# Two transformer layers on one core: transfers of the mixer's solve in a fixed order, solves and Sin moved, inverse roots of the second stage as GpSimd powers

## The chip, the cores and the metric

The kernel runs on one core of one Trainium2 chip. A core has five engines with a queue of instructions each: TensorE (PE, matmuls), VectorE (DVE), ScalarE (ACT), GpSimd (POOL) and SyncE (SP, which here only issues transfers). They meet at semaphores, and 16 DMA engines move data between DRAM and the on-chip memory. The metric is the device time of one execution in microseconds (us); lower is better. The median of three runs before is 1295.21 us (1294.62 to 1304.61).

## What is computed

512 rows of 1024 features go through two layers in fp32. The first layer mixes the sequence in two halves of the features, retention and RWKV7, then attends to a memory of 256 rows and applies a squared-ReLU MLP; the second is a gated hybrid of grouped attention and a spatial MLP. Cut to what the change touches:

```python
def wkv7_scan(r, w, k, v, a_vec, b_vec):            # 8 heads of 64, 512 steps
    def step(state, inp):
        sa = jnp.einsum('bhvk,bhk->bhv', state, a_t)
        state = (state * w_t[:, :, None, :] + sa[..., None] * b_t[:, :, None, :]
                 + v_t[..., None] * k_t[:, :, None, :])
        return state, jnp.einsum('bhvk,bhk->bhv', state, r_t)
...
def first_block(x, mem, positions, ...):
    p = rmsnorm(x, norm_mix) @ w_in
    y = concat([retention_mixer(p[:RET], positions), rwkv7_mixer(p[RET:])])   # retention turns q, k by sin, cos
    x = x + y @ w_out
    x = x + memory_cross_attention(rmsnorm(x, norm_xattn), rmsnorm(mem, norm_mem), ...)
    h = rmsnorm(x, norm_mlp)
    x = x + jnp.square(jax.nn.relu(h @ mlp_w_up)) @ mlp_w_down
    return rmsnorm(x, norm_final)

def hybrid_layer(x, ...):
    z = rmsnorm_2(x, norm_gain) @ w_in               # q, k, v, gate_a, u, v, gate_b, g_merge
    q = axial_rope(rmsnorm_2(q per head, q_gain)); k = axial_rope(rmsnorm_2(k per head, k_gain))
    attn = block_attention(q, k, v) * silu(gate_a)
    gm = gelu(u) * spatial(layernorm(gelu(v))) * silu(gate_b)
    y = sigmoid(g0) * (attn @ w_proj_attn) + sigmoid(g1) * (gm @ w_proj_gmlp)
    return x + y @ w_out                             # then a last rmsnorm_2
```

## The kernel before

**Matmuls.** Each weight unit of 128x1024 is fetched by SP (L285, `raw`), cast on ScalarE to a rounded high part `wh` (L295) and subtracted to a low part `wl` (L296) on VectorE, or on GpSimd for the units that `lowpart` names. A product takes three matmuls, high by high, high by low and low by high; most have 128x512 columns.

**Who sets the order.** TensorE's order is that in which the Python code calls `self.T` (class `Ordered` ties each instruction behind the last). The code is a main generator and side generators that `streams` runs in turns: at each `yield` the main one has emitted a step, mostly four matmuls of 128x512, and a side generator that yields n comes back n steps later. The other engines' order is set by the scheduler that places instructions.

**The mixer.** The RWKV7 half treats 512 steps as 16 chunks of 32, eight per half (`hf` 0 and 1). `side(hf)` runs `products` (chunk matrices `gs`, whose corners go through DRAM by the writes of L1595 into `dm`), `invert` (L1624: both halves of `dm` are read; L1630 and L1632: 31 elimination steps on GpSimd; L1637 to L1646: the inverse goes to DRAM as `d1` and `dw` and comes back as `sv` and as diagonal blocks of `gs`), then waits `self.wait[hf]` steps, then `solve` (two products, F and W, per half matrix, with copies on ScalarE at L1659 and L1666), then `chain`: for each chunk the xy product, the copy `xs` (L1684), steps of other matmuls, the us product, the copy L1690, and the state products. Chain 0 runs from 164 to 205 us. The `trig` generator makes sine and cosine of the retention's angles on GpSimd and ScalarE (L704); they are needed by the retention part, which follows.

**Norms.** `rsqrt` (L357 to L366) is a first guess from the bits and three Newton steps on VectorE: nine instructions for one column, twelve for several. The first stage's own row norms use one GpSimd power (`rs`, L477). Users in the change: `norm_scale` (last norm), the turn of the attention's and the MLP's rows (`turn`, L1002), `fin` at the end of the MLP (L1156 to L1170), `heads` (L1231 to L1243, ten heads of a row block) and `layer_norm` (L1291 to L1300).

Of the kernel before, what the change touches and what calls it, by code (L numbers as in the profile page):

```python
# [16 lines left out]
P = 128  # L17
# [212 lines left out]
class Kern:  # L230
    def __init__(self, ctx, tc, A, out):
        self.tc, self.nc, self.A, self.out = tc, tc.nc, A, out
        self.T = Ordered(tc, tc.nc.tensor)
        pool = lambda name, **k: ctx.enter_context(tc.tile_pool(name=name, bufs=1, **k))
        self.cp = pool("cp")
        self.wp = pool("wp")
        self.tp = pool("tp")
        self.sp = pool("sp")
        self.sm = pool("sm")
        self.dp = pool("dp", space=bass.MemoryType.DRAM)  # L240
        self.nraw = self.nspl = 0
        self.raw, self.spl = {}, {}
        self.NU = A["wst"].shape[0]
        self.u = 0
        self.cnt = 0
        self.nh = 3
        self.lowpart = lambda u: u <= 3 or 55 <= u < 79 or 145 <= u
        self.wait = [33, 25]

# [103 lines left out]
    def rsqrt(self, x, n, p0=0, p1=P, tag="sm", V=None):  # L353
# [13 lines left out]
        return y  # L367

    def rms(self, xb, junk, eps=1e-6):

        nc = self.nc
        ss = self.small(1)
        nc.scalar.activation(junk, xb, AF.Square, accum_out=ss)
        v = self.small(1)
        nc.vector.tensor_scalar(v, ss, 1.0 / D, eps, op0=ALU.mult, op1=ALU.add)
        return self.rsqrt(v, 1)
# [65 lines left out]
    def first(self):  # L442
# [29 lines left out]
        v = self.small(4)  # L472
        rs, mh = self.small(4), self.small(4)
        G.memset(mh, -0.5)
# [182 lines left out]
    def trig(self):  # L657
# [42 lines left out]
        for x, o in ((acc, self.sin), (w, self.cos)):  # L700
            V.tensor_scalar(o, x, -0.4999999, 0.4999999, op0=ALU.max, op1=ALU.min)
        yield 95
        for o in (self.sin, self.cos):
            nc.scalar.activation(o, o, AF.Sin, scale=2.0 * math.pi)  # L704

# [266 lines left out]
    def turn_half(self, st, b, j, ps, dst, delay):  # L972
# [10 lines left out]
        def turn():  # L983
# [13 lines left out]
            if b == NB - 1:  # L997
                yield 5
                v = self.small(4)
                nc.vector.tensor_reduce(v, st["ss"].rearrange("p (b j) -> p b j", j=2), axis=AX.X, op=ALU.add)  # L1000
                nc.vector.tensor_scalar(v, v, 1.0 / D, 1e-6, op0=ALU.mult, op1=ALU.add)
                st["scale"](self.rsqrt(v, 4))  # L1002

        self.spawn(turn(), delay)

    def norm_scale(self, ss, scale=1.0 / D, eps=1e-6):
        V = self.nc.vector
        v = self.small(1)
        V.tensor_reduce(v, ss, axis=AX.X, op=ALU.add)
        V.tensor_scalar(v, v, scale, eps, op0=ALU.mult, op1=ALU.add)  # L1010
        return self.rsqrt(v, 1)

# [95 lines left out]
    def mlp(self):  # L1108
# [15 lines left out]
        def main():  # L1124
# [28 lines left out]
            def fin(b):  # L1153
# [6 lines left out]
                V.scalar_tensor_tensor(c1, a1, 1.0 / D, a0, op0=ALU.mult, op1=ALU.add)  # L1160
                rs = self.rsqrt(c1, 1)
                xg = self.tmp((P, 1024), "t4", 2)
# [5 lines left out]
                self.flags.add(f"norm {b}")  # L1168
                rs = self.rsqrt(c0, 1)
                V.tensor_scalar(self.x[b], self.x[b], rs, None, op0=ALU.mult)  # L1170
# [18 lines left out]
    def second(self):  # L1189
# [32 lines left out]
        def heads(b):  # L1222
# [9 lines left out]
            V.tensor_scalar(ss, ss, 1.0 / 64, 1e-6, op0=ALU.mult, op1=ALU.add)  # L1232
            rn = self.rsqrt(ss, 10)
            V.tensor_tensor(x3, x3, rn.unsqueeze(2).broadcast_to([P, 10, 64]), op=ALU.mult)
# [53 lines left out]
        def layer_norm(b):  # L1288
# [6 lines left out]
            V.tensor_scalar(e, mv[:, 1:2], 0.25, 1e-6, op0=ALU.mult, op1=ALU.add)  # L1295
            rs = self.rsqrt(e, 1)
            V.tensor_scalar(rs, rs, 0.5, None, op0=ALU.mult)
# [274 lines left out]
    def products(self, hf, sl):  # L1572
# [7 lines left out]
        for c in range(0, 8, 2):  # L1580
# [10 lines left out]
            if c % 4 == 2:  # L1591
                q = c // 4
                for b in range(2):
                    r = 32 * b + 16 * q
                    nc.sync.dma_start(dm[r:r + 16].rearrange("p s t -> s p t"),  # L1595
                                      gs[q][32 * b:32 * b + 32, :, :, 32 * b:32 * b + 32].rearrange("s c h t -> s (c h) t"))
# [13 lines left out]
    def invert(self, hf, sl):  # L1610
# [22 lines left out]

        d1, dw = self.dram(32), self.dram()
        for e in range(2):
            o = slice(64 * e, 64 * e + 32)
            G.tensor_copy(m[o, :, 0:16], w[o].rearrange("p i t -> p t i"))  # L1637
            nc.sync.dma_start(d1[:, :, 16 * e:16 * e + 16], m[o, :, 0:16])
        for e, o in enumerate(half):
            nc.sync.dma_start(dw.rearrange("p (i e) t -> p i e t", e=2)[:, :, e], w[o])  # L1640
        sv = m[0:32]
        nc.sync.dma_start(sv, d1.rearrange("p t c -> t p c"))
        for b in range(2):
            for q in range(2):
                r = 32 * b + 16 * q
                nc.sync.dma_start(gs[q][32 * b:32 * b + 32, :, :, 32 * b:32 * b + 32].rearrange("s c h t -> s (c h) t"),  # L1646
                                  dw[r:r + 16].rearrange("p c t -> c p t"))
        sl["fw"] = sv, m[32:64]

    def solve(self, hf, sl):  # L1650
# [11 lines left out]
        for q in range(2):  # L1662
            wp = self.psum("cs", (32, 16, 32))
            for i in range(16):
                self.T.matmul(wp[:, i], f[:, q * 16 + i], gs[q][32:64, i // 4, i % 4, 32:64], start=True, stop=True)
            SC.copy(gs[q][0:32, :, :, 32:64], wp.rearrange("p (c h) t -> p c h t", h=4))  # L1666
        yield 2

    def chain(self, hf, sl):
# [5 lines left out]
        for c in range(8):  # L1675
# [8 lines left out]
            SC.copy(xs, xy[0:64])  # L1684
            yield 2
            us = self.psum("ch")
# [64 lines left out]
```

## Time and profile before

| what | before |
|---|---|
| runs (us) | 1304.61, 1295.21, 1294.62; median 1295.21 |
| profiled execution (us) | 1293.28, of which the span is 1291.5 |
| TensorE busy | 1243.6 us (96%), 6976 instructions |
| VectorE, ScalarE, GpSimd busy | 690.8 (53%), 511.2 (40%), 455.5 us (35%) |
| mean granted clock of TensorE | 0.988 of full speed |
| mixer / attention and MLP / second layer | 0 to about 390 / to 930 / to 1291 us |

The time is that of one profiled execution. An engine is busy while an instruction of it runs; a wait is the idle time ahead of an instruction, put down to what released it. TensorE has two clock levels, 1.2 and 2.4 GHz, and the granted clock of a stretch is the mean over it as a share of 2.4 GHz.

### The profile page before, as it was taken

To read this page: it belongs to the slowest core of one execution; us is meant where nothing else is said; L and a number is where in the kernel's file an instruction comes from. 1 tells how busy PE (TensorE), PEld (TensorE's weight loads), DVE (VectorE), ACT (ScalarE), POOL (GpSimd) and SP (SyncE) were. 2 spreads that over 40 slices of the span, in tenths; PEclk is the share of its full clock that TensorE was granted. 3 is DMA by queue.
4 is the path that set the end of the run, shared out by engine and by line. 5 is a ranking of instruction groups with operands and counts; after the bars stand their busy time and mean duration, and the time that the engine had idled before them with its cause. 6 is when DMAs were issued, how large, how long until landed. Compare 5 with 4: busy or idle time off the path is not lost.

```text
span 1291.5 us, 18137 instructions
## 1 busy us (share of the span) xinstructions
PE 1243.6 (96%) x6976; PEld 1027.9 (80%) x6976; DVE 690.8 (53%) x1455; ACT 511.2 (40%) x921; POOL 455.5 (35%) x490
## 2 busy tenths in 40 slices
PE   7999699999999999999999999999999999999997
PEld 6767578887888898798888888888787878787886
DVE  5767323557784555444333333334869856564455
ACT  5453133332354544444322232234444435455232
POOL 5917572244210242235210111012314763222574
PEclk9999799999999999999999999999999999999999
DMA  6222414111245232223333323243232231221321
GB/s 207 75 57 82 98 43 109 50 37 63 90 139 187 60 97 82 82 66 114 98 98 98 95 91 96 96 123 97 93 98 65 83 114 51 64 66 50 114 82 66
DMA packets 52089, 115.49 MB, mean 89 GB/s; under 512 B 23169, under 2 KB 23809, under 8 KB 52002
## 3 DMA queue, kind: packets, MB, share of 16 engines
q1 hardware_dynamic: 51824, 114.25, 29.6%
q8 instruction: 55, 0.90, 0.3%
q14 instruction: 32, 0.26, 0.1%
q10 hardware_dynamic: 146, 0.07, 0.0%
q0 software_dynamic: 32, 0.00, 0.0%
HBM read 110.90 MB, written 3.41 MB: 89 GB/s over the span
## 4 chain that ended last, share of the span: by engine, by line
PE 79%; POOL 7%; DVE 6%; ACT 4%; issue 2%; DMA 2%; SPq 0%; ACTq 0%; DVEq 0%; POOLq 0%
PE mm L221 36%; PE cs L221 32%; PE ch L221 7%; PE tp L221 4%; POOL s L221 3%; POOL o L1630 1%; POOL s L1632 1%; ACT wh L295 1%; DVE wl L296 1%; DMA raw<-wst 1%; DMA s<-dm 1%; DVE s L887 1%; ACT t L1102 0%; DVE t L1104 0%; DMA dm<-s 0%
## 5 line engine op out<-in xcount | busy, mean ns | idle before, releaser
L221 PE MATMUL mm<-s,wh 128*128 128x512 f32 (+1 forms) x880 | 263.3, 379 | 2.2 <-DVE t L542 2.0
L295 ACT CAST wh<-raw 128x1024 fp32r<-128x1024 f32 x151 | 158.6, 1051 | 255.8 <-PE mm L221 197.8
L221 PE MATMUL mm<-wh,s 128*128 128x512 f32 (+1 forms) x824 | 229.2, 347 | 1.2 <-DVE t L719 0.8
L296 DVE TENSOR_TENSOR wl<-raw,wh 128x1024 fp32r<-128x1024 f32 x99 | 123.2, 1244 | 171.3 <-ACT wh L295 170.8
L221 PEld LDWEIGHTS mm<-s,wh 128*128 128x128 f32 x880 | 159.0, 190 | 37.5 <-issue 7.2
L296 POOL TENSOR_TENSOR wl<-raw,wh 128x1024 fp32r<-128x1024 f32 x52 | 125.7, 2420 | 134.5 <-ACT wh L295 123.2
L221 PEld LDWEIGHTS mm<-wh,s 128*128 128x128 f32 x824 | 146.5, 191 | 22.1 <-PE mm L221 1.2
L221 PE MATMUL mm<-s,wl 128*128 128x512 f32 (+1 forms) x432 | 163.1, 378 | 1.0 <-DVE wl L221 1.0
L221 PE MATMUL cs<-s,wh 128*128 128x512 f32 (+1 forms) x544 | 154.2, 366 | 0.0
L221 PE MATMUL mm<-wl,s 128*128 128x512 f32 (+1 forms) x412 | 140.7, 342 | 2.5 <-POOL wl L296 2.5
L221 PE MATMUL cs<-wh,s 128*128 128x512 f32 (+1 forms) x440 | 143.0, 389 | 0.0
L1120 POOL TENSOR_TENSOR t<-t 128x512 f32<-128x512 f32 x32 | 49.9, 1559 | 217.0 <-ACT t L1119 217.0
L221 PEld LDWEIGHTS cs<-s,wh 128*128 128x128 f32 x544 | 97.8, 189 | 16.2 <-issue 0.2
L221 PE MATMUL cs<-s,wl 128*128 128x512 f32 (+1 forms) x272 | 99.7, 366 | 0.0
L221 PEld LDWEIGHTS cs<-wh,s 128*128 128x128 f32 x440 | 82.5, 190 | 16.4
L221 PEld LDWEIGHTS mm<-s,wl 128*128 128x128 f32 x432 | 81.8, 189 | 14.7 <-DVE wl L221 1.2
L296 POOL TENSOR_TENSOR wlx<-raw,whx 128x1024 fp32r<-128x1024 f32 x17 | 41.3, 2428 | 136.4 <-ACT whx L295 133.2
L221 PEld LDWEIGHTS mm<-wl,s 128*128 128x128 f32 x412 | 78.9, 191 | 11.5 <-POOL wl L296 2.9
L221 PE MATMUL cs<-wl,s 128*128 128x512 f32 (+1 forms) x220 | 85.5, 389 | 0.0
L351 DVE TENSOR_TENSOR s<-t,s 128x512 fp32r<-128x512 f32 x44 | 34.8, 790 | 64.1 <-ACT s L350 64.0
L221 PE MATMUL ch<-s,s 128*64 128x64 f32 (+3 forms) x504 | 61.1, 268 | 4.8 <-ACT s L1690 2.4
L295 ACT CAST whx<-raw 128x1024 fp32r<-128x1024 f32 x35 | 36.6, 1047 | 66.4 <-PE mm L221 48.1
(312 smaller groups left out, 2128.6 us busy)
## 6 DMA issues: line engine op xcount, KB each, us to landing
raw<-wst SPq DMA_DIRECT2D x189, 512.0 KB, 3.7
s<-x SPq DMA_DIRECT2D x8, 512.0 KB, 5.7
s<-rows SPq DMA_DIRECT2D x4, 512.0 KB, 4.2
out<-t SPq DMA_DIRECT2D x8, 256.0 KB, 2.3
t<-mem SPq DMA_DIRECT2D x2, 512.0 KB, 3.9
dm<-s SPq DMA_DIRECT2D x10, 64.0 KB, 2.3
s<-dm SPq DMA_DIRECT2D x2, 256.0 KB, 4.1
s<-dm SPq DMA_DIRECT2D x8, 64.0 KB, 2.5
```

The source lines that it names most:

```text
L221: r = getattr(self.eng, name)(*a, **k)
L295: (SC or nc.scalar).copy(h, r)
L296: (E or (nc.gpsimd if self.lowpart(self.nspl) else nc.vector)).tensor_tensor(l, r, h.bitcast(F32), op=ALU.subtract)
L351: self.nc.vector.tensor_tensor(dst[1], src, dst[0].bitcast(F32), op=ALU.subtract)
L887: (V or self.nc.vector).tensor_tensor(dst[1], ps, dst[0].bitcast(F32), op=ALU.subtract)
L1120: nc.gpsimd.tensor_tensor(q, r, r, op=ALU.mult)
L1630: G.tensor_tensor(tv, w[:, 0:k, s:s + 1].broadcast_to([P, k, n]), m[:, s:s + 1, s + 1:32].broadcast_to([P, k, n]), op=ALU.mult)
L1632: G.tensor_tensor(w[:, 0:k, s + 1:32], w[:, 0:k, s + 1:32], tv, op=ALU.add)
```

## The change

- `self.wait` becomes [40, 16]: solve 0 starts seven steps later behind its products, solve 1 nine steps earlier.
- The Sin and Cos of L704 wait for the flag "solve 0" and are tied behind the last copy of the W product.
- The chunk writes of L1595 go to ScalarE's queue, in the order of the code.
- The transfers around the inverse are issued on SP in a fixed order: both `dw`, both `d1`, two reads of diagonal blocks, `sv`, two reads.
- In half 0 the chain yields one step fewer between `xs` and the us product.
- `power` replaces `rsqrt` at 22 places outside the mixer: a GpSimd `tensor_tensor` with the operation pow and a tile of -0.5.

```diff
-        self.wait = [33, 25]
+        self.wait = [40, 16]
...
+    def power(self, x, n):
+        y = self.small(n)
+        self.nc.gpsimd.tensor_tensor(y, x, self.half[:, 0:n], op=ALU.pow)
         return y
...
-        rs, mh = self.small(4), self.small(4)
+        rs = self.small(4)
+        mh = self.half = self.cp.tile([P, 10], F32, name="half")
         G.memset(mh, -0.5)
...
         yield 95
+        yield "solve 0"
         for o in (self.sin, self.cos):
-            nc.scalar.activation(o, o, AF.Sin, scale=2.0 * math.pi)
+            r = nc.scalar.activation(o, o, AF.Sin, scale=2.0 * math.pi)
+            self.tc.add_manual_dep(r.ins, self.mark.ins.name, mybir.DependencyInfo(
+                mybir.DependencyClass.NoSync, mybir.DependencyReason.DATA), reason="order of the instructions")
...
-                st["scale"](self.rsqrt(v, 4))
+                st["scale"](self.power(v, 4))
...
-                rs = self.rsqrt(c1, 1)
+                rs = self.power(c1, 1)
...
-            rn = self.rsqrt(ss, 10)
+            rn = self.power(ss, 10)
...
-                    nc.sync.dma_start(dm[r:r + 16].rearrange("p s t -> s p t"),
+                    SC.dma_start(dm[r:r + 16].rearrange("p s t -> s p t"),
...
+        Q = Ordered(self.tc, nc.sync)
+        for e, o in enumerate(half):
+            Q.dma_start(dw.rearrange("p (i e) t -> p i e t", e=2)[:, :, e], w[o])
         for e in range(2):
             o = slice(64 * e, 64 * e + 32)
             G.tensor_copy(m[o, :, 0:16], w[o].rearrange("p i t -> p t i"))
-            nc.sync.dma_start(d1[:, :, 16 * e:16 * e + 16], m[o, :, 0:16])
-        for e, o in enumerate(half):
-            nc.sync.dma_start(dw.rearrange("p (i e) t -> p i e t", e=2)[:, :, e], w[o])
+            Q.dma_start(d1[:, :, 16 * e:16 * e + 16], m[o, :, 0:16])
         sv = m[0:32]
-        nc.sync.dma_start(sv, d1.rearrange("p t c -> t p c"))
         for b in range(2):
             for q in range(2):
...
-                nc.sync.dma_start(gs[q][32 * b:32 * b + 32, :, :, 32 * b:32 * b + 32].rearrange("s c h t -> s (c h) t"),
+                Q.dma_start(gs[q][32 * b:32 * b + 32, :, :, 32 * b:32 * b + 32].rearrange("s c h t -> s (c h) t"),
...
+            if b == 0:
+                Q.dma_start(sv, d1.rearrange("p t c -> t p c"))
...
-            SC.copy(gs[q][0:32, :, :, 32:64], wp.rearrange("p (c h) t -> p c h t", h=4))
+            self.mark = SC.copy(gs[q][0:32, :, :, 32:64], wp.rearrange("p (c h) t -> p c h t", h=4))
...
             SC.copy(xs, xy[0:64])
-            yield 2
+            yield 1 + hf
```

The same replacement of `rsqrt` by `power` stands in `norm_scale`, in `fin` for c0 and in `layer_norm`. Line numbers of the kernel after are larger by 6 to 12.

**SP at solve 0.** `dm_1004` is `dw` of half 0, `dm_1003` its `d1`, `s_156_904` (after: `s_155_904`) the tile that holds `sv`, and `s_126`, `s_127` (`s_125`, `s_126`) are the two chunk matrices. First SP's row before:

```order
L1640 DMA dm_1004<-s_156_904 1024x1x32 x2
L1638 DMA dm_1003<-s_156_904 1024x1x16
L1646 DMA s_126_757<-dm_1004 32x16x32
L1646 DMA s_127_758<-dm_1004 32x16x32
L1646 DMA s_126_757<-dm_1004 32x16x32
L1638 DMA dm_1003<-s_156_904 1024x1x16
L1646 DMA s_127_758<-dm_1004 32x16x32
L1595 DMA dm_1294<-s_240_1292 32x16x32 x2
L1642 DMA s_156_904<-dm_1003 32x32x32
```

Now, in the changed kernel:

```order
L221 DMA dm_1004<-s_155_904 1024x1x32 x2
L221 DMA dm_1003<-s_155_904 1024x1x16 x2
L221 DMA s_125_757<-dm_1004 32x16x32
L221 DMA s_126_758<-dm_1004 32x16x32
L221 DMA s_155_904<-dm_1003 32x32x32
L221 DMA s_125_757<-dm_1004 32x16x32
L221 DMA s_126_758<-dm_1004 32x16x32
L285 DMA raw_1519<-wst 128x1024
```

Both parts of `d1` moved ahead of the reads, `sv` ahead of the last two, and the writes for the second half (L1595) left SP's row. TensorE's row at the same place, before, with the F matmuls of solve 0 (`cs_1526`, `cs_1544`):

```order
L221 MATMUL mm_1349<-s_12_106,wh_1241 128x512
L221 MATMUL mm_1349<-s_14_108,wh_1241 128x512
L221 MATMUL mm_1349<-s_12_106,wl_1242 128x512
L221 MATMUL cs_1526<-s_156_904,s_126_757 32x32 x16
L221 MATMUL cs_1544<-s_156_904,s_127_758 32x32 x16
L221 MATMUL mm_1525<-s_11_105,wh_1282 128x512
```

and now (`cs_1564`, `cs_1582`):

```order
L221 MATMUL mm_1525<-s_12_106,wl_1282 128x512
L221 MATMUL mm_1559<-s_11_105,wh_1345 128x512
L221 MATMUL mm_1559<-s_13_107,wh_1345 128x512
L221 MATMUL mm_1559<-s_11_105,wl_1346 128x512
L221 MATMUL mm_1559<-s_11_105,wh_1345 128x512
L221 MATMUL cs_1564<-s_155_904,s_125_757 32x32 x16
L221 MATMUL cs_1582<-s_155_904,s_126_758 32x32 x16
```

The 24 matmuls into `mm_1525` and four into `mm_1559` moved ahead of the solve.

**ScalarE from solve 0 to chunk 0.** Before, the row from the W copies (L1666) to the copy of the us product (L1690):

```order
L1666 COPY s_126_757<-cs_1570 32x16x32
L1666 COPY s_127_758<-cs_1588 32x16x32
L1684 COPY xs_1619<-ch_1614 64x256
L1606 COPY s_308_1621<-cs_1622 128x4x128
L1606 COPY s_308_1621<-cs_1628 128x4x128
L295 CAST wh_1647<-raw_1343 128x1024
L764 ACTIVATE t_1642<-mm_1525 128x512
L1690 COPY s_42_280<-ch_1652 64x256
```

Now, the same stretch (L1678 are the W copies, L1696 `xs`, L1702 the copy of the us product):

```order
L1678 COPY s_126_758<-cs_1626 32x16x32
L712 ACT_TABLE_LOAD
L712 ACTIVATE sin<-sin 128x128
L712 ACTIVATE cos<-cos 128x128
L1696 COPY xs_1657<-ch_1652 64x256
L1616 COPY s_312_1659<-cs_1660 128x4x128
L1616 COPY s_312_1659<-cs_1666 128x4x128
L295 CAST wh_1681<-raw_1519 128x1024
L774 ACT_TABLE_LOAD
L774 ACTIVATE t_1676<-mm_1559 128x512
L1702 COPY s_41_280<-ch_1688 64x256
```

Sin, Cos and two table loads came in; the three loads that stood further ahead, around L704, L1467 and L1459, are gone from the row.

**GpSimd at `heads`.** `L1242` and `L1243` (after: L1252 and L1253) make the rotated queries and keys of a row block. Before:

```order
L1242 TENSOR_TENSOR s_1390_8233<-t_1470_8687,t_1471_8688 128x20x16
L1243 TENSOR_TENSOR s_1390_8233<-t_1470_8687,t_1471_8688 128x20x16
L296 TENSOR_TENSOR wl_8766<-raw_8647,wh_8765 128x1024
L296 TENSOR_TENSOR wlx_8836<-raw_8717,whx_8835 128x1024
L1242 TENSOR_TENSOR s_1391_8234<-t_1490_8803,t_1491_8804 128x20x16
L1243 TENSOR_TENSOR s_1391_8234<-t_1490_8803,t_1491_8804 128x20x16
L296 TENSOR_TENSOR wl_8883<-raw_8763,wh_8882 128x1024
```

Now:

```order
L1252 TENSOR_TENSOR s_1377_8167<-t_1445_8555,t_1446_8556 128x20x16
L1253 TENSOR_TENSOR s_1377_8167<-t_1445_8555,t_1446_8556 128x20x16
L296 TENSOR_TENSOR wl_8634<-raw_8528,wh_8633 128x1024
L372 TENSOR_TENSOR sm_8655<-sm_8652,half 128x10
L296 TENSOR_TENSOR wlx_8691<-raw_8585,whx_8690 128x1024
L1252 TENSOR_TENSOR s_1378_8168<-t_1463_8658,t_1464_8659 128x20x16
L1253 TENSOR_TENSOR s_1378_8168<-t_1463_8658,t_1464_8659 128x20x16
L296 TENSOR_TENSOR wl_8738<-raw_8631,wh_8737 128x1024
```

The power of row block 2 stands ahead of a weight split, `wlx`, and the split that follows the queries keeps its place.

## Rows read from the trace of the kernel before

**Rows 1.** TensorE's waits, 60 to 320 us: waiter, released by, total us, times, longest

```profile
PE cs L221 <- DMA s<-dm: 9.4, 1, 9.4
PE ch L221 <- ACT s L1690: 2.4, 3, 1.1
...
PE mm L221 <- DVE t L542: 2.0, 1, 2.0
```

**Rows 2.** TensorE's waits, 900 to 1292 us

```profile
PE tp L221 <- DVE t L1165: 2.5, 1, 2.5
PE mm L221 <- POOL wl L296: 2.5, 1, 2.5
```

**Rows 3.** Windows: stretch, length; busy us of PE, PEld, DVE, ACT, POOL; clock, DMA share, GB/s

```profile
60.00:80.00 20.00, 18.05 (x86) 13.44 (x84) 13.56 (x20) 11.91 (x17) 6.98 (x12) 0.91 0.26 73
...
180.00:200.00 20.00, 17.79 (x158) 14.45 (x156) 11.54 (x25) 6.42 (x15) 16.02 (x34) 1.00 0.30 70
...
900.00:950.00 50.00, 46.73 (x213) 37.79 (x212) 38.34 (x128) 21.62 (x57) 13.20 (x25) 0.97 0.28 84
950.00:1000.00 50.00, 47.53 (x260) 40.77 (x259) 42.03 (x103) 21.45 (x37) 17.59 (x12) 1.00 0.32 102
```

**Rows 4.** Timeline of GpSimd: start, us, engine, line, operation, out<-in

```profile
141.91 2.24 POOL L1637 COPY s<-s 32x512 f32<-32x512 f32 x2
```

**Rows 5.** Timeline of SP: issues

```profile
145.72 1.39 SPq L1646 DMA_DIRECT2D s<-dm  x3
...
148.54 1.03 SPq L1595 DMA_DIRECT2D dm<-s  x2
```

**Rows 6.** Chain that ended last, 100 to 175 us: start, us, what

```profile
147.21 2.51 DMA dm<-s
149.73 2.74 DMA s<-dm
152.61 3.59 PE cs L221 x64
156.20 3.71 PE mm L221 x8
...
165.00 1.02 PE cs L221 x8
166.02 1.84 PE mm L221 x8
167.86 0.60 PE ch L221 x8
```

**Rows 7.** Timeline of ScalarE, 56 to 76 us

```profile
69.05 1.28 ACT L704 ACT_TABLE_LOAD   x1
```

**Rows 8.** Timeline of ScalarE, 164 to 206 us; in brackets idle time ahead

```profile
165.74 1.08 ACT L1606 COPY s<-cs 128x512 f32<-128x512 f32 x2 [0.34 <-PE cs L221]
167.67 1.04 ACT L295 CAST wh<-raw 128x1024 fp32r<-128x1024 f32 x1 [0.85 <-PE mm L221]
...
169.11 0.35 ACT L1690 COPY s<-ch 64x256 f32<-64x256 f32 x1
```

**Rows 9.** GpSimd's groups of one line and shape: busy us, mean ns, idle

```profile
L221 POOL TENSOR_TENSOR sm<-sm,sm 128x1 f32<-128x1 f32 x4 | 2.2, 556 | 8.2 <-DVE sm L221 8.2
```

**Rows 10.** Timeline of VectorE, 920 to 933 us

```profile
923.40 0.15 DVE L1160 SCALAR_TENSOR_TENSOR sm<-sm,sm 128x1 f32<-128x1 f32 x1
...
930.61 1.40 DVE L1165 SCALAR_TENSOR_TENSOR t<-s,sm,s 128x512 f32<-128x512 f32 x2
```

**Rows 11.** Timeline of VectorE, 955 to 992 us

```profile
979.26 2.37 DVE L364 TENSOR_TENSOR sm<-sm 128x10 f32<-128x10 f32 x1
```

**Rows 12.** Timeline of GpSimd, 918 to 1030 us

```profile
988.57 2.35 POOL L296 TENSOR_TENSOR wl<-raw,wh 128x1024 fp32r<-128x1024 f32 x1
```

**Rows 13.** Chain that ended last, 1280 to 1292 us

```profile
1287.05 0.17 DVE sm L366
```

**Rows 14.** Timeline of GpSimd, 1240 to 1292 us

```profile
1284.13 1.40 POOL L970 TENSOR_TENSOR t<-s,s 128x256 f32<-128x256 f32 x2 [2.42 <-DVE s L954]
```

More of the change, by code (lines that the diff above doesn't have):

```diff
@@ L367, in rsqrt @@
         return y
+    def power(self, x, n):
+        y = self.small(n)
+        self.nc.gpsimd.tensor_tensor(y, x, self.half[:, 0:n], op=ALU.pow)
+        return y
     def rms(self, xb, junk, eps=1e-6):
@@ L1010, in norm_scale @@
         V.tensor_scalar(v, v, scale, eps, op0=ALU.mult, op1=ALU.add)
-        return self.rsqrt(v, 1)
+        return self.power(v, 1)
     def x1(self):
@@ L1168, in fin @@
                 self.flags.add(f"norm {b}")
-                rs = self.rsqrt(c0, 1)
+                rs = self.power(c0, 1)
                 V.tensor_scalar(self.x[b], self.x[b], rs, None, op0=ALU.mult)
@@ L1295, in layer_norm @@
             V.tensor_scalar(e, mv[:, 1:2], 0.25, 1e-6, op0=ALU.mult, op1=ALU.add)
-            rs = self.rsqrt(e, 1)
+            rs = self.power(e, 1)
             V.tensor_scalar(rs, rs, 0.5, None, op0=ALU.mult)
@@ L1645, in invert @@
                 r = 32 * b + 16 * q
-                nc.sync.dma_start(gs[q][32 * b:32 * b + 32, :, :, 32 * b:32 * b + 32].rearrange("s c h t -> s (c h) t"),
-                                  dw[r:r + 16].rearrange("p c t -> c p t"))
+                Q.dma_start(gs[q][32 * b:32 * b + 32, :, :, 32 * b:32 * b + 32].rearrange("s c h t -> s (c h) t"),
+                            dw[r:r + 16].rearrange("p c t -> c p t"))
+            if b == 0:
+                Q.dma_start(sv, d1.rearrange("p t c -> t p c"))
         sl["fw"] = sv, m[32:64]
```

## The prediction

> **What bounds the kernel now.** I read the list of TensorE's waits first, since TensorE works almost without a break: a change can only win the time in which it stands still or runs at its lower clock. By far the longest wait is 9.4 us for the transfers into the chunk matrices, in front of solve 0. In the mixer there are then three waits for the copy of L1690 in the chain, 2.4 us together and 1.1 at most, and 2.0 us for the token shift of L542 [rows 1]; in the second half of the program 2.5 us for a normed row block of `fin` (L1165) and 2.5 us for a weight split on GpSimd [rows 2]. The windows say what a wait costs beyond its length: around the one of 2.0 us the mean granted clock is 0.91 of 2.4 GHz over 20 us, so 1.8 us were lost at 1.2 GHz; around L1165's it is 0.97 over 50 us, 1.5 us lost; around the GpSimd split's it is 1.00, and so it is from 180 to 200 us, where the waits are near 1 us [rows 3]. So a wait of 2 us or more often costs another 1.5 to 1.8 us, one of 1 us does not.
>
> Third, the chain of work through solve 0. GpSimd has the inverse at 141.9 us and copies its two halves until 144.2 [rows 4]. Three reads of the diagonal blocks are issued on SP from 145.7 on, in 1.39 us [rows 5]; the second half of `d1` comes behind them, at 147.2, and lands 2.5 us later. Only then is `sv` read, in 2.7 us, and the F matmuls start at 152.6, at half speed: the eight matmuls of 128x512 behind them take 3.71 us, the same number ten us later 1.84 [rows 6].
>
> **The change part by part.** The sum is made against the profiled execution, 1293.28 us, which is 1.9 us under the median of 1295.21.
>
> *Solve 0 later, its transfers in a fixed order.* The order shows 28 matmuls of 128x512 more ahead of solve 0. At 1.84 / 8 = 0.23 us [rows 6] they last 6.4 us, so TensorE, which now stands still from 143.2 (152.6 - 9.4), would come to the solve at 149.6. The data come earlier too: `d1`'s second half now stands ahead of the reads, so it is issued when GpSimd's copy ends, at 144.2 [rows 4], and lands by 146.7; `sv` takes 2.7 us from there [rows 6] and the last two reads, behind it, two issues of 0.46 [rows 5] more: 149.4 to 150.4. So 0 to 1 us of the wait stays; I take 0.8. The half-speed stretch goes with the wait: 3.59 for the F matmuls and 3.71 for the eight behind them [rows 6] are about twice what the work needs, 3.6 us. Together -(9.4 - 0.8) - 3.6 = **-12.2** (bounds -9 and -13.5). The chunk writes on ScalarE's queue take a pair of issues, 1.03 us, out of SP's row between the last read and `sv` [rows 5]; that is contained in this. ScalarE issues them in stretches where it waits for TensorE, so I cost them at nothing; without that cover it is 8 issues of 0.5 us, and what stands behind them is a weight cast. Solve 1, two steps earlier in the order, has no wait now [rows 1], and its inverse starts earlier by more than those 1.8 us, since its chunk writes no longer queue on SP.
>
> *Sin and Cos behind solve 0.* ScalarE now loads a table for Sin, waits for the angle, loads back and loads a third time, 1.28 us each, just ahead of the tanh that L542 needs [rows 7]. The order takes all that away, and with it the wait: -2.0, and -1.8 of clock: **-3.8** (bounds 0 and -3.8). Two loads and the two activations come back between solve 0 and chunk 0.
>
> *Chain 0.* Two things work against the change there: the second of these loads stands ahead of chunk 0's L1690 copy, and each of the eight chunks of half 0 has a step (four matmuls, 0.92 us) less between the xs copy and the us matmuls. For chunk 0 ScalarE has, behind the xs copy (0.35, and 0.34 idle), the L1606 pair 1.08, the weight cast 1.04, the load 1.28, and tanh and copy, which end 0.75 us behind the cast [rows 7, 8]: 4.8 us. TensorE has until then eight transposes, eight matmuls and the us product: 3.5 us [rows 6]. So it waits 1.4 us, with the hand-over about 1.7, perhaps with a loss of clock (half of 1.8). One wait like the 1.1 us of today, where cast and tanh stand ahead of the copy, will remain. 1.7 + 0.9 + 1.1 - 2.4 = **+1.3**. Bounds: -2.4 if all these waits go, and 8 x 1.1 + 0.9 - 2.4 = +7.3 if every chunk gets one.
>
> *Powers instead of Newton steps.* The only power in the trace, 128x1, takes 0.556 us [rows 9]. For 128x4 and 128x10 the bounds are 0.55 and ten times 0.556, 5.6 us; I take 0.8 and 1.5, nearer to the row, as estimates. *fin:* the sum of row block 2 is ready at 923.55, but the small instructions of three row blocks take turns on VectorE with weight splits, and L1165 starts at 930.61 [rows 10]. The power stands ahead of twelve L1228 products on GpSimd, so it can end near 924.2, and L1165 is ready long before TensorE asks: **-4.0** (2.5 [rows 2] and 1.5 of clock). *heads, block 2:* a Newton step on VectorE, 0.17 us where it has the memory to itself [rows 13], takes 2.37 us at 979.26 [rows 11], beside a GpSimd split; with eleven more of about 0.2 us the chain lasts 4.6 us. The split that TensorE waits for starts at 988.57 [rows 12], behind the rotated queries of this block. If the power takes p and the product behind it (0.8 us) is stretched by 1.5 us, to about as long as that step, this split starts 3.1 - p earlier, 1.6 us at p = 1.5 (2.5 at 0.55, and 2.5 later at 5.6). Two layer norms then stand ahead of a later split, for which TensorE does not wait now [rows 2]; I charge 0.3: **-1.3**. *Tail:* GpSimd ends L970 at 1285.53 [rows 14] and the power by 1286.1, where the last Newton step ends at 1287.22 [rows 13]: **-1.1**. The powers of attention and MLP feed scores and scales that TensorE does not wait for [rows 2]: nothing.
>
> GPSIMD Engine Reference of the Trainium skill, section "Engine selection", speaks against this part: it gives elementwise work to VectorE, GpSimd being about twice as slow on two inputs. The rows here differ from it for 128x1, where one instruction stands for nine that wait for their turn; for the wide powers the rule would point to the third rival.
>
> Sum: -12.2 - 3.8 + 1.3 - 4.0 - 1.3 - 1.1 = -21.1 us, 1272.2 for the profiled execution, **1274 us** on the scale of the median.
>
> **Rivals.** (a) *The chain gives half back.* Every chunk of half 0 waits about 1.1 us, and two more waits are long enough for the lower clock: +7.3 + 2 x 1.8 instead of +1.3, so 1274 + 9.6 = 1284. For it: a step less in every chunk, and three such waits today [rows 1]. Against: five of the eight chunks show no wait for that copy today [rows 1], and the clock holds with waits of about 1 us [rows 3]. (b) *The solve still waits.* If the data come 4 us after TensorE, the lower clock stays too: 3.2 + 3.6 us back, 1281, and 1284 with half of (a). Against: three issues less stand ahead of `d1` [rows 5]. (c) *Wide powers cost by the column.* At 5.6 us the four of `heads` turn 1.3 us won into 2.5 lost at each: 1.3 + 4 x 2.5 = 11 us, 1285. (d) *The other side:* chain 0 falls to the lower clock for good. If a chunk's wait grows to 2 us or more, a low stretch can follow in every chunk. Chain 0 lasts from 164 to 205 us, and TensorE is busy for 17.8 of 20 us in it [rows 3], so half speed throughout costs up to 36 us: 1274 + 36 = 1310. It decides at 2 us per chunk. Against: matmuls at half speed take twice as long and so cover the copy, which ends such waits. (e) *The powers change nothing for TensorE:* 6.4 us less won, 1280.
>
> **How the numbers follow.** Forecast 0.50 and (e) 0.10; (a) 0.12, (b) 0.11, (c) 0.08, (d) and what is like it 0.09. 1% is 13 us, about what a measurement of this kernel can tell from no change, so under 1282 is faster. The forecast, (e) and half of (b) are there: 0.65. The rest of (b), (a) and (c) are within 1%: 0.26. Slower: 0.09. The range reaches down to all gains at their bounds (1274 - 1.3 - 3.7 - 1.2 = 1268) less the loss of a clock stretch or two by chance, 1263; up over (a) to (c) to 1289.
>
> **What the profile after would show.** At solve 0 at most 1 us of idle time, and a clock of 1.00 between 140 and 180 us. No table load near 65 us and no wait for L542. Two loads around chunk 0 and one wait of 1.7 us for L1690. No wait for L1165 at the end of the MLP. Powers of 128x4 under 1 us and of 128x10 under 2 us. I am wrong if `sv` or a diagonal block lands more than 2 us after TensorE is there, if most chunks of chain 0 show a wait or a low clock, or if the wide powers take over 3 us.

## The result and the profile after

The changed kernel takes 1279.15 us (median of four runs, 1272.75 to 1281.54); runs of the kernel before beside them have a median of 1294.91. The ratio is 0.986, with a 95% interval of 0.983 to 0.990: 1.4% faster, 15.8 us where 21 were forecast. The time lies inside the range given. The profiled execution takes 1280.32 us, with a span of 1278.6 us and a mean granted clock of 0.988, the same as before. TensorE is busy for 97% of it; VectorE fell from 690.8 to 654.0 us, GpSimd rose from 455.5 to 473.0 us.

TensorE's waits after, 60 to 320 us and then 900 to 1279 us (waiter, released by, us in all, times, longest), answering [rows 1, 2]:

```profile
PE ch L221 <- DVE st L1718: 2.5, 3, 0.9
PE ch L221 <- ACT s L1702: 2.4, 2, 1.3
PE mm L221 <- DVE kt L775: 2.1, 1, 2.1
PE mm L221 <- DVE t L729: 2.0, 1, 2.0
PE ch L221 <- DVE gs L1738: 1.6, 1, 1.6
```

```profile
PE ch L221 <- DVE s L897: 1.7, 4, 1.1
PE mm L221 <- POOL wl L296: 1.6, 1, 1.6
```

The 9.4 us for the transfers into the solve are gone, and so are the 2.0 us for the token shift (L542) and the 2.5 us for `fin` (L1165). The GpSimd split still costs 1.6 us. New is 2.1 us for L775: a VectorE product whose input comes from ScalarE's tanh, L774. The wait for L729 has grown, from two of 0.4 us to one of 2.0. The chain of work through the solve, 100 to 175 us (start, us, what), answering [rows 6]:

```profile
140.22 1.13 POOL s L1650
141.36 2.49 DMA dm<-s
143.93 0.35 ACTq L1605
144.32 0.58 ACTq L1605
145.00 1.06 ACT wh L295
146.09 0.69 DVE wl L296
147.23 0.69 DVE kt L775
147.96 1.29 PE mm L221 x4
149.26 3.55 PE cs L221 x64
152.80 3.41 PE mm L221 x8
```

GpSimd's copy, the second part of `d1`, ScalarE's two issues of the second half's chunk writes (L1605), a weight cast on ScalarE behind them, VectorE, TensorE. The solve no longer waits for its data; it waits for ScalarE, and the F matmuls run at half speed once more (3.55 us, before 3.59). The windows show it (length; busy us of PE, PEld, DVE, ACT, POOL; clock; DMA share; GB/s), answering [rows 3]:

```profile
60.00:80.00 20.00, 20.00 (x108) 14.47 (x106) 15.11 (x21) 9.14 (x14) 8.38 (x13) 1.00 0.27 79
140.00:160.00 20.00, 17.86 (x173) 14.65 (x172) 3.55 (x4) 6.45 (x9) 7.76 (x19) 0.83 0.67 153
900.00:950.00 50.00, 48.93 (x275) 41.66 (x274) 32.16 (x59) 24.62 (x56) 20.00 (x32) 1.00 0.31 100
950.00:1000.00 50.00, 48.39 (x222) 39.59 (x221) 36.90 (x62) 25.34 (x39) 33.09 (x22) 1.00 0.26 75
```

At Sin and at `fin` the clock is now 1.00; at the solve it is 0.83 over 20 us.

**A measure for the comparisons.** From its lowest to its highest of eight runs, the changed kernel's time varies by 9.4 us, the product of its span and its mean granted clock by 4.1 (standard deviations 3.3 and 1.4). That product, here called the *full-clock span*, is the time that the core would have needed if its lower-clock stretches had run at full clock (idle time inside them counts half); span minus product is *lost to the clock*. The first separates kernels that the time alone doesn't: over the four chips used, its mean for the kernel before is 1274.8 to 1275.3. It is not free of the clock, though: among the runs of one kernel it falls by some 0.2 us for each us more that is lost to the clock (0.22 over the 42 runs of before), so kernels that lost different amounts compare to about 1 us, and the clock, recorded to three digits, leaves 0.6 us either way in each run. All runs of the study, with the runs of before that stood beside the experiments:

| kernel | runs | median us (range) | ratio to before [95%] | full-clock span, mean | lost to the clock, mean |
|---|---|---|---|---|---|
| before | 42 | 1294.2 (1289.2–1306.6) | | 1275.1 | 19.3 |
| after, both labels | 8 | 1280.6 (1272.8–1282.2) | 0.986 [0.983, 0.990] | 1262.4 | 15.2 |
| only_power | 10 | 1289.7 | 0.997 [0.994, 0.999] | 1271.2 | 16.6 |
| no_power | 6 | 1283.2 | 0.992 [0.989, 0.995] | 1266.0 | 15.6 |
| sp_q1 | 4 | 1277.9 | 0.989 [0.985, 0.994] | 1264.4 | 13.1 |
| lane_dummy | 4 | 1275.5 | 0.986 [0.983, 0.989] | 1262.9 | 10.5 |
| sin_back | 4 | 1274.8 | 0.985 [0.979, 0.991] | 1265.3 | 9.3 |
| chain_two | 4 | 1278.0 | 0.987 [0.982, 0.992] | 1263.6 | 12.1 |
| wait_back | 10 | 1290.7 | 0.996 [0.992, 1.000] | 1269.0 | 20.0 |
| sp_writes | 4 | 1277.1 | 0.986 [0.980, 0.991] | 1263.8 | 11.5 |
| order_back | 4 | 1281.6 | 0.987 [0.982, 0.992] | 1263.7 | 15.7 |
| lane42 | 4 | 1274.8 | 0.983 [0.978, 0.987] | 1265.6 | 8.0 |
| lane41 | 4 | 1270.8 | 0.980 [0.975, 0.985] | 1259.1 | 9.8 |

(The ratio of the second row is that of the first label; the other, after_again, has 0.986 with 0.981 to 0.992.)

### The profile page after: what moved, and what is told of

The parts are those of the page before. It is cut to its first block, busy times and chain, and to the rows that moved or that the text cites. A ratio compares the mean times of both kernels' runs of the same rounds, so it can differ in the third digit from the quotient of the medians.

```text
span 1278.6 us, 17927 instructions
## 1 busy us (share of the span) xinstructions
PE 1244.9 (97%) x6976; PEld 1030.4 (81%) x6976; DVE 654.0 (51%) x1239; ACT 508.8 (40%) x919; POOL 473.0 (37%) x512
## 3 DMA queue, kind: packets, MB, share of 16 engines
HBM read 110.90 MB, written 3.41 MB: 89 GB/s over the span
## 4 chain that ended last, share of the span: by engine, by line
PE 85%; DVE 5%; POOL 4%; ACT 3%; DMA 1%; issue 1%; ACTq 0%; POOLq 0%; DVEq 0%; SPq 0%
PE mm L221 40%; PE cs L221 33%; PE ch L221 8%; PE tp L221 4%; POOL o L1640 1%; POOL s L1642 1%; ACT wh L295 1%; DVE wl L296 1%; POOL s L1238 1%; ACT t L1112 0%; DVE t L1114 0%; DVE st L1718 0%; DVE s L221 0%; DVE s L897 0%; DMA s<-dm 0%
## 5 line engine op out<-in xcount | busy, mean ns | idle before, releaser
L221 PE MATMUL mm<-wh,s 128*128 128x512 f32 (+1 forms) x824 | 233.6, 352 | 3.8 <-DVE t L729 2.0
```

The costliest lines, as they stand in the source:

```text
L221: r = getattr(self.eng, name)(*a, **k)
```

## The experiments

### The two parts of the change, apart

**only_power**: the kernel before with the 22 powers alone. One of the six replacements, and the function added:

```diff
+    def power(self, x, n):
+        y = self.small(n)
+        self.nc.gpsimd.tensor_tensor(y, x, self.half[:, 0:n], op=ALU.pow)
+        return y
...
-                rs = self.rsqrt(c1, 1)
+                rs = self.power(c1, 1)
```

> The kernel before with the 22 powers of GpSimd alone, mixer untouched. Theory (the powers take away the wait for L1165 and most of the wait for a GpSimd split, and shorten the tail): 5 to 7 us faster than before, no wait for L1165 near 929 us, a span of about 1285. Rival (TensorE is not held by the norms, the gain is all in the mixer): within 1.5 us of before. The wait of 9.4 us at solve 0 stays in both.

**no_power**: the changed kernel with `rsqrt` at these places again.

```diff
-                rs = self.power(c1, 1)
+                rs = self.rsqrt(c1, 1)
```

> The changed kernel with Newton steps in place of the powers, so the mixer's part alone. Theory (parts add): 8 to 10 us faster than before, with the waits of 2.5 us near 920 and 977 us back. Rival (the mixer's gain is lost again behind it): within 3 us of before.

The powers are worth 3.9 us of full-clock span on the kernel before (1275.1 to 1271.2) and 3.6 on the changed mixer (1266.0 to 1262.4); the mixer's part is worth 9.1 (1275.1 to 1266.0) and 8.8 (1271.2 to 1262.4). So the parts add up. By the time, only_power gains 4.5 us (the ratio 0.9965) where 5 to 7 were expected, and its wait for the GpSimd split is still 1.8 us; no_power gains 10.6 (0.9918) where 8 to 10 were. In no_power the two waits of the second half come back, in its list of TensorE's waits, 900 to 1285 us:

```profile
PE mm L221 <- POOL wl L296: 2.4, 1, 2.4
PE tp L221 <- DVE t L1175: 2.4, 1, 2.4
```

And what the powers cost stands in GpSimd's groups of the changed kernel (line, operation, form, count | busy us, mean ns | idle before), answering [rows 9]:

```profile
L372 POOL TENSOR_TENSOR sm<-sm,half 128x1 f32<-128x1 f32 x16 | 8.9, 567 | 7.4 <-DVE sm L1170 5.8 <-DVE sm L1305 1.5
L372 POOL TENSOR_TENSOR sm<-sm,half 128x10 f32<-128x10 f32 x4 | 7.9, 1965 | 21.1 <-DVE sm L1242 21.0
L372 POOL TENSOR_TENSOR sm<-sm,half 128x4 f32<-128x4 f32 x2 | 2.1, 1032 | 0.2
```

The three widths lie on a line: 0.41 us and 0.155 us for each column.

### Who holds ScalarE up

In the changed kernel ScalarE computes nothing for 8.72 us ahead of the cast that TensorE's wait goes back to (its timeline, 128 to 172 us: start, us, engine, line, what; in brackets the time ahead without computing, the issues in it counted):

```profile
135.65 0.63 ACT L1561 ACTIVATE kt<-t 32x512 f32<-32x512 f32 x1 [2.01 <-DVE t L549]
143.93 0.98 ACTq L1605 DMA_DIRECT2D dm<-s  x2
145.00 1.05 ACT L295 CAST wh<-raw 128x1024 fp32r<-128x1024 f32 x1 [8.72 <-DMA s<-dm]
146.08 0.60 ACT L774 ACTIVATE t<-mm 128x512 f32<-128x512 f32 x1
```

The products that these two writes carry were ready at 138.55 us, by VectorE's timeline:

```profile
137.26 1.29 DVE L1599 TENSOR_TENSOR s<-cs,cst 128x512 f32<-128x512 f32 x2 [0.40 <-PE cs L221]
```

So of the 8.72 us, 2.3 were a wait for the data and 1.0 the issues; in the 5.4 us between them, the writes waited for something else. ScalarE's row of the program, with the semaphores that each instruction waits for:

```
L1605 DMA dm_1294<-s_240_1293 32x16x32 [waits DMAHW7_49,DVE_49]
L1605 DMA dm_1294<-s_240_1293 32x16x32 [waits DMAHW0_49]
L295 CAST wh_1521<-raw_1280 128x1024 [waits DMAHW1_49,PE_49]
L774 ACTIVATE t_1516<-mm_1349 128x512 [waits PE_49]
```

This program's transfers signal their end on eight semaphores, taken in turn by SP's and ScalarE's transfers together in the order in which the scheduler placed them, and the program lets a transfer be issued only when the one before it on its semaphore has landed. The first write of half 1's second pair shares DMAHW7 with the second part of `d1`, eight places ahead, on SP; the trace's records, too, have these two on one semaphore. That part is issued at 141.3 and lands at 143.85 (141.36 + 2.49 in the chain); ScalarE goes on at 143.93. The theory: a transfer of the other queue holds ScalarE up by a shared semaphore, and the cast and the tanh are queued behind it. The rival: ScalarE is late through its own work or for its data.

**sp_q1**: only that pair of writes goes back to SP.

```diff
-                    SC.dma_start(dm[r:r + 16].rearrange("p s t -> s p t"),
+                    (nc.sync if hf and q else SC).dma_start(dm[r:r + 16].rearrange("p s t -> s p t"),
```

> The changed kernel with one pair of the chunk writes, the second of half 1, back on SP. Theory (ScalarE stands from 136 to 144 us because this pair waits on its queue for the semaphore that the second d1 transfer holds): ScalarE's casts of 145.0 and 146.6 us come at their data, 8 and 4 us earlier, TensorE's wait of 2.15 us for L775 goes, solve 0 then waits 1 to 1.5 us for its last read; with a clock stretch less 2 to 5 us faster than the changed kernel. Rival (the cast waits for its weights, or the tanh for TensorE): ScalarE's rows and the wait of 2.15 us stay as they are.

ScalarE casts at 138.50 and makes the tanh at 139.58; neither L775 nor the solve shows a wait. But SP issues the pair only at 144.23, inverse 1 starts at 155.78 instead of 153.89, and its GpSimd steps now stand ahead of a product of chain 0. From the timeline of that run, 167 to 175 us:

```profile
171.65 0.98 POOL L1715 TENSOR_TENSOR su<-st,pc 64x128 f32<-64x128 f32 x2
172.08 0.28 DVE L1718 TENSOR_TENSOR st<-sc,su 64x128 f32<-64x128 f32 x1 [5.50 <-POOL su L1715]
173.10 1.19 PE L221 MATMUL ch<-st,s 128*128 128x128 f32 x4 [5.34 <-DVE st L1718]
```

A wait of 5.34 us for GpSimd takes the place of 2.15: the full-clock span rises by 2.0. The cause of the wait is confirmed, and another limit is uncovered: from the second pair through inverse 1 to the chain. The median of the time is 2.7 us lower than the changed kernel's, but on four runs from 1275.6 to 1285.9 us; the 2 to 5 us expected are not shown.

**lane_dummy**: the pair stays on ScalarE but gets other semaphores. Half 1's writes are placed behind `d1`, and one transfer of 64 bytes on SP is put between the two writes of the pair. (`dep` ties its first instruction behind its second in the scheduler's order.)

```diff
-                    SC.dma_start(dm[r:r + 16].rearrange("p s t -> s p t"),
+                    w = SC.dma_start(dm[r:r + 16].rearrange("p s t -> s p t"),
...
+                    if hf:
+                        dep(w, self.d1w)
+                    if hf and q:
+                        if b:
+                            dep(w, self.shift)
+                        else:
+                            self.shift = nc.sync.dma_start(self.cp.tile([1, 16], F32, name="shift"), self.A["rows"][0:1, 0:16])
+                            dep(self.shift, w)
...
-            Q.dma_start(d1[:, :, 16 * e:16 * e + 16], m[o, :, 0:16])
+            self.d1w = Q.dma_start(d1[:, :, 16 * e:16 * e + 16], m[o, :, 0:16])
```

> The changed kernel with all chunk writes on ScalarE, but the scheduler's order of transfers shifted so that the last pair of half 1 shares its semaphores with the first pair and no longer with d1 and a read; one small extra transfer on SP is added for that. Theory (the shared semaphore is what holds ScalarE): the pair is issued near 138.6 us, right behind its products, and ScalarE's stall of 8.7 us goes with TensorE's 2.15 us; inverse 1 starts by 149 instead of 153.9; 2 to 5 us faster than the changed kernel. Rival (ScalarE's queue of transfers, or data that come late, hold it): the pair is still issued near 144 us.

The same instructions on the same engine, and ScalarE's stall is gone (its timeline, 134 to 148 us):

```profile
135.12 0.63 ACT L1561 ACTIVATE kt<-t 32x512 f32<-32x512 f32 x1 [2.70 <-DVE t L549]
137.45 0.85 ACTq L1605 DMA_DIRECT2D dm<-s  x2
138.48 0.60 ACT L774 ACTIVATE t<-mm 128x512 f32<-128x512 f32 x1 [2.73 <-PE mm L221]
138.97 1.04 ACT L295 CAST wh<-raw 128x1024 fp32r<-128x1024 f32 x1
```

That settles the semaphore against the rival. The F matmuls start at 146.87 us instead of 149.26, but now the data are late (TensorE's timeline, 140 to 165 us, and the window of the solve, with a lower clock than in the changed kernel, 0.86):

```profile
146.87 2.54 PE L221 MATMUL cs<-s,s 32*32 32x32 f32 x64 [2.08 <-DMA s<-dm]
```

```profile
140.00:165.00 25.00, 22.92 (x197) 18.46 (x196) 3.47 (x4) 8.57 (x15) 12.45 (x30) 0.73 0.52 114
```

The full-clock span stays as in the changed kernel (1262.9); the 5 us by which the median of the time is lower are all in the clock, and its four runs lie within the changed kernel's range. I had expected inverse 1 to start by 149; it starts at 153.01, since SP issues the read of the pair's data at 146.14, behind the reads of the solve. So the wait of L775 and the wait for the data covered each other: taking one away exposes the other.

**lane42** and **lane41**: lane_dummy, with solve 0 two steps later, or one.

```diff
-        self.wait = [40, 16]
+        self.wait = [42, 16]
```

> The kernel lane_dummy with solve 0 two steps later still. Theory (its wait of 2.08 us at solve 0 is the last read landing after TensorE is there): eight matmuls, 1.84 us, cover it, at most 0.4 us are left and no low clock between 145 and 160 us; span times mean granted clock 1 to 2 us under the 1262.9 of lane_dummy. Rival (chain 0 then waits for inverse 1 on GpSimd, or the work is missing later): the wait comes back behind the solve and the product stays.

> lane_dummy with solve 0 one step later instead of two. Theory: four matmuls, 0.92 us, leave about 1.1 us of the wait of 2.08 us at solve 0, too short for the long low clock that followed it; a time like that of lane42, 1273 to 1278. Rival (what lane42 won is the scatter of the clock): 1278 to 1283, like the changed kernel.

In lane42 the solve waits no more and only 8.0 us are lost to the clock, the least of all; but chain 0 waits 2.5 us for its state (L1728) at 168.95, and the full-clock span is 2.7 us above lane_dummy's where 1 to 2 less were expected: a miss. Two of its waits, 60 to 320 us:

```profile
PE ch L221 <- DVE st L1728: 4.8, 4, 2.5
PE ch L221 <- DVE gs L357: 2.0, 1, 2.0
```

In lane41 the solve waits 1.05 us and keeps its clock (TensorE's waits, 60 to 320 us, and the window of the solve; the same window of the changed kernel behind it):

```profile
PE ch L221 <- DVE st L1728: 5.8, 3, 3.4
PE ch L221 <- ACT xs L1706: 1.5, 2, 1.0
PE cs L221 <- DMA s<-dm: 1.1, 1, 1.1
PE mm L221 <- DVE t L729: 0.8, 2, 0.4
```

```profile
140.00:165.00 25.00, 22.96 (x246) 18.49 (x245) 5.11 (x7) 11.81 (x20) 12.76 (x29) 1.00 0.56 133
```

```profile
140.00:165.00 25.00, 22.53 (x206) 17.90 (x204) 4.73 (x5) 10.83 (x16) 12.08 (x28) 0.86 0.54 122
```

It is the fastest kernel of the study: 1270.8 us, 2.0% below before, and its full-clock span is 3.3 us below the changed kernel's, with no run in the other's range (1258.1 to 1259.5 against 1260.5 to 1264.6). Between the two the intervals of the ratio to before overlap; the full-clock span parts them. By the timelines, TensorE's waits from 60 to 400 us add up to 10.0 us in lane41, 12.2 in lane_dummy and 14.7 in lane42, which is the order of their full-clock spans. Of the 2.5 us that lane42 waits more than lane_dummy, 0.7 stand ahead of 250 us and 1.8 behind, so chain 0 alone does not tell why two steps lose. Why the waits fall so is not tested, and neither is the one step later without the other semaphores.

### The other edits of the mixer, undone one by one

**sp_writes**: all chunk writes on SP's queue.

```diff
-                    SC.dma_start(dm[r:r + 16].rearrange("p s t -> s p t"),
+                    nc.sync.dma_start(dm[r:r + 16].rearrange("p s t -> s p t"),
```

> The changed kernel with all chunk writes back on SP; the order of code lets one pair of half 1 stand between the two d1 transfers there. Theory (SP issues in its row's order and ScalarE is free): no stall of ScalarE near 140 us and no wait for L775; the reads of the diagonal blocks and sv come some 1 us later behind those writes, so solve 0 waits 1 to 3 us; within 4 us of the changed kernel either way. Rival (the move to ScalarE's queue is worth the wait that SP's row had): over 5 us slower.

1277.1 us, full-clock span 1.4 above after: no difference in time that can be measured. ScalarE doesn't stall, the solve waits 0.68 us, and the chain 4.28 us for its state, as in sp_q1. Moving the writes to ScalarE's queue gained next to nothing, which fits: there they wait for a semaphore, as on SP for their turn.

**order_back**: the transfers around the inverse in the order of before.

```diff
-            Q.dma_start(d1[:, :, 16 * e:16 * e + 16], m[o, :, 0:16])
+            nc.sync.dma_start(d1[:, :, 16 * e:16 * e + 16], m[o, :, 0:16])
...
+        nc.sync.dma_start(sv, d1.rearrange("p t c -> t p c"))
...
-            if b == 0:
-                Q.dma_start(sv, d1.rearrange("p t c -> t p c"))
```

> The changed kernel with the transfers around the inverse in the order of before (the second d1 behind three reads, sv last), solve 0 still seven steps later. Theory: sv is read some 3 us later than in the changed kernel, near 151 us, so solve 0 waits 1 to 3 us more than it does now, mostly with a longer low clock: span times mean granted clock 1 to 4 us above the 1262.6 of the changed kernel. Rival (the later solve alone hides the transfers): within 1 us of 1262.6.

`sv` is now issued at 145.01, and still no wait for data shows at the solve: the wait for L775, 3.3 us here, covers it. The full-clock span is 1.3 us higher, about what the measure can tell, so the fixed order is worth little while ScalarE is the later of the two.

**wait_back**: solve 0 at its old distance; solve 1 stays at 16. (The second number of `self.wait` was not undone by itself.)

```diff
-        self.wait = [40, 16]
+        self.wait = [33, 16]
```

> The changed kernel with solve 0 at its old place, 33 steps behind its products. Theory (28 matmuls, 6.4 us, are what hides the transfers): TensorE waits 5 to 7 us for the last read at solve 0, the lower clock follows it, and the kernel is 4 to 9 us slower than the changed one. Rival (the order of the transfers alone hides them): a wait under 2 us and no slower than the changed one.

TensorE waits 6.5 us for the data and the clock is low for two long stretches (list of waits, 60 to 320 us; windows):

```profile
PE cs L221 <- DMA s<-dm: 6.5, 1, 6.5
```

```profile
140.00:180.00 40.00, 33.52 (x299) 26.46 (x297) 5.61 (x10) 14.66 (x26) 19.72 (x45) 0.74 0.33 76
200.00:230.00 30.00, 27.67 (x256) 25.47 (x257) 5.57 (x13) 6.84 (x16) 2.70 (x3) 0.60 0.25 63
```

6.6 us of full-clock span and 4.8 of clock, 11.4 together, where 4 to 9 were expected: the seven steps alone are most of what the mixer's part gains.

**chain_two**: two steps between `xs` and the us product in half 0 again.

```diff
-            yield 1 + hf
+            yield 2
```

> The changed kernel with the chain of half 0 as before, one step more between the xs copy and the us product. Theory (the shorter chain costs only the two waits of 1.33 and 1.04 us seen for L1702): between 3 us faster and 3 us slower than the changed kernel. Rival (a) of the prediction (each chunk of the shorter chain waits): over 5 us faster.

The two waits for L1702 go, and with them 1.6 us for L1738 and 2.0 for L729; others come (one of 2.4 us for L1718, 2.5 for L897, 2.6 for L1748 at 375 us). The full-clock span is 1.2 us higher, and no difference in the time can be told. The step fewer is not a loss.

**sin_back**: Sin and Cos where they were.

```diff
-        yield "solve 0"
         for o in (self.sin, self.cos):
-            r = nc.scalar.activation(o, o, AF.Sin, scale=2.0 * math.pi)
+            nc.scalar.activation(o, o, AF.Sin, scale=2.0 * math.pi)
```

> The changed kernel with Sin and Cos where they were, not behind solve 0. Theory: the wait of 2.0 us for L549 near 72 us is back and mostly a stretch at the lower clock with it, 3.4 to 4.4 us in the first 100 us; the table load at chunk 0 goes and with it most of the wait of 1.33 us for L1702. Together 1 to 3 us slower than the changed kernel. Rival (the table loads behind solve 0 cost the chain as much): no difference, or faster.

The 1.9 us wait for the token shift comes back, and with it 2.9 us of full-clock span, about 1.8 at an equal loss of clock. But three of the four runs lost little to the clock (0.995 to 0.997), and the median is below the changed kernel's, where 1 to 3 us more were expected. So the wait is worth about its own 2 us; whether the edit helps the time isn't shown. Four runs don't tell if that clock is the edit's doing or chance.

### What the clock does by itself

**after_again**: the changed kernel, unchanged.

> The changed kernel once more, beside the others on one chip. Theory (the scatter of a kernel's runs is the clock that its waits of 1.5 to 2.2 us lose in one run and not in another): span times mean granted clock again 1261 to 1264, while the time goes from 1271 to 1282 with the clock. Rival (the scatter has another source): the product scatters as the time does.

The full-clock span is 1261.2 to 1263.6, the time 1276.9 to 1282.2: what differs between runs is mostly the clock. The traces show it. In its first trace, the changed kernel waits 1.97 us at 281.96 and 1.85 us at 364.20 (for L729 and L897) and loses clock at both; sp_q1 has the same two waits and loses none. Windows of after, then of sp_q1:

```profile
280.00:300.00 20.00, 18.03 (x129) 15.94 (x128) 14.82 (x36) 7.01 (x13) 9.25 (x14) 0.91 0.17 53
360.00:380.00 20.00, 18.15 (x89) 14.94 (x89) 14.26 (x36) 11.85 (x23) 2.09 (x2) 0.91 0.55 169
```

```profile
280.00:300.00 20.00, 17.95 (x125) 14.16 (x124) 15.64 (x39) 6.80 (x13) 10.02 (x15) 1.00 0.21 73
360.00:380.00 20.00, 18.15 (x84) 14.66 (x83) 15.65 (x30) 13.64 (x24) 1.75 (x2) 1.00 0.58 176
```

And the 1.13 us wait at 1092.74 costs a stretch in the first trace of the changed kernel and none in after_again. First after, then after_again:

```profile
1090.00:1110.00 20.00, 18.21 (x79) 14.27 (x78) 10.64 (x25) 9.24 (x19) 4.81 (x2) 0.91 0.20 54
```

```profile
1090.00:1110.00 20.00, 18.20 (x88) 14.45 (x87) 12.37 (x29) 10.03 (x20) 4.80 (x2) 1.00 0.18 53
```

## Why the prediction was right, and where not

How far ahead of before the same-numbered matmul of TensorE starts, in the two profiled executions, gives each step:

| step | forecast us | measured us |
|---|---|---|
| ahead of 60 us (not touched) | 0 | +1.6 |
| Sin and Cos moved | -3.8 | -4.4 |
| solve 0, chain 0, rest of the mixer | -12.2 + 1.3 = -10.9 | -6.6 |
| `fin` | -4.0 | -3.3 |
| `heads` | -1.3 | -0.9 |
| around 1094 us (not touched) | 0 | +1.9 |
| tail | -1.1 | -1.2 |
| sum | -21.1 | -12.9 |

**Right.** The waits named for Sin and `fin` went, with their clock, and the tail shrank, each by about what its rows said. Chain 0 has just the two waits for L1702 that were forecast as 1.7 and 1.1 us: 1.33 and 1.04. Rival (a) falls by this and by chain_two; (d) needed 2 us in each chunk; (e) falls by only_power and no_power; (c) needed 5.6 us for a 128x10 power, which takes 1.97. Rival (b) was nearest: the solve still waited over 2 us and ran at half speed. But its condition, data later than TensorE, was not met.

**The step that failed** is the sentence "ScalarE issues them in stretches where it waits for TensorE, so I cost them at nothing", on the chunk writes. The issues themselves are cheap, 0.98 us a pair, as the prediction had them (0.5 us each). Left out was that an engine which issues a transfer stands still until that transfer may start, with all that is queued behind it. In the kernel before, this pair was issued on SP at 150.88 us, 9.5 us after its products were ready (141.37), and nothing stood behind it there but transfers; on ScalarE a cast and a tanh stood behind it. The order shown ahead of the prediction lists ScalarE from the solve on, not the writes before it, and the semaphores that they wait for were not looked at. The price: 2.15 us of wait instead of 0.8, and the half-speed stretch of 7.3 us [rows 6] hardly shrank (3.55 + 3.41 = 7.0), so the 3.6 us of clock did not come: together about +4.7 of the 8.2 that the profiled pair lacks.

The Trainium skill, DMA: Bandwidth & Descriptors, section "Issuing engines are not separate DMA queues", says that starting transfers from several engines saves only the sequencer's time to start them. sp_writes agrees: without ScalarE's queue the ratio to before is the same, 0.986. How long the issuing engine stands for such a transfer is another matter; here it stood 5.4 us beyond its data.

**A rule too simple** was "a wait of 2 us or more often costs another 1.5 to 1.8 us, one of 1 us does not". It was read from one execution [rows 3]. A wait of the same length loses a stretch in one run and none in the next, at 1.1 us as at 2.0. The profiled run after has three such stretches between 240 and 390 us, where before had one, while the waits from 215 to 390 us are 7.1 us against 7.7 by the timelines: +3.4 by chance or nearly so, as are the two untouched stretches at the start and at 1094 us. The kernel before has two more waits of the mixer of some 2 us, which the prediction passed over (60 to 320 us):

```profile
PE ch L221 <- DVE gs L357: 2.0, 1, 2.0
PE ch L221 <- DVE st L1706: 1.9, 1, 1.9
```

Each has a low stretch behind it (clock 0.84 from 270 to 280 us and 0.83 from 200 to 210 us), and both are gone from the changed kernel, whose own of that length stand at L729 and L897. In the mean over all runs the change gains 12.7 us of full-clock span, against 15.1 forecast in waits and tail, and 4.1 us of clock, against 6.0: the mean clock did better than this one trace. Of the mixer's step, -10.9 + 4.7 + 3.4, less 2.2 because chain 0 waits 0.9 us less than before (1.33 + 1.04 + 0.83 against 1.05 + 1.17 + 1.88) instead of 1.3 more, leaves -5.0 (these 2.2 are luck: the waits for L1706 and L1726 that shrank stand in no term of the forecast); of the 1.6 to the measured -6.6, another 0.6 is the shorter waits behind 215 us, and 1.0 stays unassigned.

**Mis-sized terms.** The wide power: 1.5 us taken, 1.97 measured; so 3.1 - 1.97 = 1.1 was to be had at `heads`, and the split's wait fell by 2.5 - 1.6 = 0.9. The 128x4: 0.8 taken, 1.03 measured, behind which nothing waits. The lower bound for the solve, -13.5, is 0.5 more than its terms give (9.4 + 3.6 = 13.0). The Trainium skill's rule from the GPSIMD Engine Reference, section "Engine selection", which gives elementwise work to VectorE, does not decide here, where one power stands for nine to twelve VectorE instructions: no_power is 3.6 us slower in full-clock span.

## What to carry to other kernels

Before a transfer is moved to the queue of an engine that computes, read what the issue waits for, its completion semaphore too, and what is queued behind it; that wait becomes the engine's own. When two waits end at nearly the same moment, taking one away shows only the other: here the solve's data, ScalarE and inverse 1 lay within 2 us of each other, and one step of distance beside the semaphore's mending gave what the mending alone did not. Compare kernels by span times granted clock beside the time when effects of 2 to 5 us are at stake.

## What the runs showed that was not expected

- A pair of transfers that takes 0.98 us to issue held ScalarE 5.4 us beyond its data, through a semaphore shared with another engine's queue; one transfer of 64 bytes between the two, with the writes placed behind `d1`, ended it.
- Over 42 runs of the kernel before, the time spans 17.5 us and the full-clock span 4.7 (1272.4 to 1277.1): most of the scatter is TensorE's clock, and waits of 1.1 to 2.0 us, equal to 0.1 us between runs, lose about 1.7 us of clock or nothing.
- A GpSimd power costs 0.41 us plus 0.155 us a column of 128 partitions, from 1 to 10 columns (0.567, 1.032 and 1.965 us).
